# First feed-forward matrix as seven half-size products, its granules alternating in pairs with those of the second matrix

## The chip, the cores and the metric

The kernel runs on one core of one Trainium2 chip. The metric is device time in microseconds (us) of one execution: 1838.39 us as the median of three runs (1836.11 to 1846.52). All durations below come from one profiled execution, which took 1839.03 us in all and whose instructions span 1837.2 us. The engines are TensorE (PE; its weight loads stand apart as PEld), VectorE (DVE), ScalarE (ACT), GpSimd (POOL) and SyncE (SP, which here only issues DMAs).

## The reference, cut to what matters

One step of a decoder trunk runs on 256 prompt rows and 32 sample rows, so 288 columns in all (`N`), with a model width of 2048. After three recurrent branches and their merge, the last part is a feed-forward layer, and almost half of the kernel's time goes there:

```python
xn = rmsnorm(x, P['g_norm2']) * (1.0 + sc2) + sh2
x = x + gt2 * (jnp.square(jax.nn.relu(xn @ P['w_ff1'])) @ P['w_ff2'])
y = rmsnorm(x, g_final)
```

`w_ff1` is 2048 by 8192, `w_ff2` is 8192 by 2048, both float32. `gt2` is one of six vectors that the conditioning product `silu(c) @ w_ada + b_ada` yields.

## The kernel before

**Precision.** Every float32 matrix and every activation is split into two float16 parts, hi and lo, and a product is made of three float16 products: hi·hi, hi·lo and lo·hi. A weight's hi is written by ACT (a scaled copy), its lo by DVE (`rest`, L134: a scalar_tensor_tensor that reads the raw float32 and the hi, both in SBUF). `rest` also leaves a mark (a sum over its outputs) from which `certificates` later tell whether the fast program is accurate enough; the second copy of the program, behind `tc.If`, is not run.

**Granules.** Weights come in granules of 128 x 1024 float32 (512 KB, one DMA on SP's queue). A granule of the first matrix is 4 row tiles by 256 output columns, one of the second is 2 row tiles by 512. Four granules make a `Block`; each granule is 24 matmuls of 128 x 128 weights against 288 columns (8 tile products times 3). Each matrix has 32 blocks, so there are 256 granules and 6144 matmuls, all at L301.

**Order.** The hidden layer is cut into eight parts (`hb`) of 1024 features. The blocks run ff1(0), ff1(1), ff2(0), ff1(2), ff2(1) and so on: ff1 has four blocks a part, ff2 four more that add into `facc` (`a`, tiles s6 and s7). `feed_forward` goes through the granules ("visits"; the first eight in pairs). At each visit it emits the conversion (hi, lo) of the granule `depth` = 5 further on, then the 24 matmuls of this one, then, where a block ends, its evacuation: for ff1 relu, square and split (L1916 to L1918 and L134), for ff2 the addition to `facc` on DVE (L1940). Inside `in_order` the queues of PE, ACT and DVE keep exactly the order of the code. `convert` also issues the DMA for the granule that takes over the raw buffer it has just read (nine buffers). SP's queue is in program order. POOL is placed by the scheduler.

**Beside it.** The 16 remaining units of the GT2 conditioning product (`gt0`, `gt1`) are worked off during the stage by `every`: "L" loads 1 MB, "C" splits half of it on ACT and DVE (L449, L134), "v" multiplies it on PE (L466). When ff2(6) ends, POOL scales `facc` by gt2 and adds it to x (`half_resid`, L1924 to L1927), so that the last block only adds its own share. Check sums (`certify`) run on DVE and PE at several points.

## Time and profile before

| what | us |
|---|---|
| median of three runs | 1838.39 |
| the profiled execution, in all | 1839.03 |
| its span, first to last instruction | 1837.2 |
| feed-forward, first to last matmul of L301 | 768.0 (1052.7 to 1820.7) |
| PE busy in the span | 1770.3 (96%) |
| DVE busy in the span | 1204.6 |
| ACT busy in the span | 914.6 |
| POOL busy in the span | 216.5 |

A row of a group reads: line, engine, operation, output<-inputs, shape, count, then busy time in us and the mean of one in ns, then the engine's idle time just ahead of them and what ended it. The busy time of a PE group counts overlap once; the mean of one matmul (286 ns) holds its passage through the array, so the distance between two starts is read from a timeline row.

### The profile page before, as it was taken

Reading aid. Unit: us, or ns where it says so; the run is one execution under the profiler, and the core shown is the slowest. Engines: PE = TensorE matmul, PEld = TensorE weight load, DVE = VectorE, ACT = ScalarE, POOL = GpSimd, SP = SyncE. Lnnn points to the kernel's source line nnn. Section 1 sums busy time; section 2 is a strip of 40 time slices with the busy share of each in tenths; the row PEclk is TensorE's granted clock in tenths of the full one; section 3 lists DMA queues with packets and bytes.
Section 4 is the critical chain, followed back from the end, with each engine's and each line's share of the span. In section 5 each row is a group of like instructions: output and inputs, shape, how many; then the busy total and the mean of one; then the engine's idle time right before and its main releaser. Section 6 shows DMA issues by size and latency. Waiting matters only on the chain.

```text
span 1837.2 us, 38589 instructions
## 1 busy us (share of the span) xinstructions
PE 1770.3 (96%) x15792; PEld 1376.8 (75%) x15792; DVE 1204.6 (66%) x2603; ACT 914.6 (50%) x1268; POOL 216.5 (12%) x281
## 2 busy tenths in 40 slices
PE   7999989998898999999999899999999999999996
PEld 5787667786677877677777677777777777777785
DVE  4777855646787467777767776556665666555565
ACT  5334374555455455465556555554444444343443
POOL 0002201110125010001113510000000000000171
PEclk9999999999999999999999999999999999999998
DMA  9999766647755459977778546566656655555541
GB/s 393 414 409 335 260 227 247 216 157 247 237 194 187 163 196 297 323 259 252 254 271 316 221 165 204 201 200 220 203 197 206 216 198 197 179 177 181 180 154 54
DMA packets 113291, 422.97 MB, mean 230 GB/s; under 512 B 11649, under 2 KB 11937, under 8 KB 109905
## 3 DMA queue, kind: packets, MB, share of 16 engines
q1 hardware_dynamic: 97744, 364.18, 56.7%
q0 software_dynamic: 10608, 39.64, 6.3%
q10 hardware_dynamic: 4752, 16.60, 2.4%
q8 instruction: 125, 2.05, 0.4%
q14 instruction: 62, 0.50, 0.1%
HBM read 403.56 MB, written 16.81 MB: 229 GB/s over the span
## 4 chain that ended last, share of the span: by engine, by line
PE 63%; DVE 2%; DMA 2%; issue 1%; ACT 1%; POOL 0%; DVEq 0%; POOLq 0%; ACTq 0%
PE mm L301 32%; PE mm L237 19%; PE pi L301 8%; PE pa L466 1%; DMA st<-mC 1%; DMA o_C_s<-st 1%; DVE pair L134 0%; PE px L1629 0%; PE px L1639 0%; PE px L1715 0%; DVE st L1718 0%; PE pi L1698 0%; DMA xl<-wf 0%; DVE s L2051 0%; PE px L1570 0%
## 5 line engine op out<-in xcount | busy, mean ns | idle before, releaser
L237 PEld LDWEIGHTS <-pair 128*128 128x128 f16 x6528 | 633.1, 98 | 218.3 <-issue 36.1
L301 PEld LDWEIGHTS <-pair 128*128 128x128 f16 x6144 | 600.8, 98 | 160.2 <-issue 8.3
L237 PE MATMUL mm<-x,pair 128*128 128x288 f16 x4320 | 563.7, 287 | 14.1 <-ACT s L714 6.1
L134 DVE SCALAR_TENSOR_TENSOR pair<-raw,pair 128x1024 f16<-128x1024 f32 x250 | 308.3, 1235 | 213.7 <-ACT pair L224 119.5
L301 PE MATMUL mm<-hx,pair 128*128 128x288 f16 x2472 | 321.0, 286 | 0.0
L301 PE MATMUL mm<-z,pair 128*128 128x288 f16 x2448 | 312.7, 287 | 4.4 <-ACT z L1899 3.7
L134 DVE SCALAR_TENSOR_TENSOR pair<-xl,pair 128x1024 f16<-128x1024 f32 x165 | 202.7, 1229 | 132.6 <-ACT pair L224 73.3
L224 ACT ACTIVATE pair<-raw 128x1024 f16<-128x1024 f32 x163 | 171.5, 1054 | 202.3 <-PE mm L237 118.9
L134 DVE SCALAR_TENSOR_TENSOR pair<-s,pair 128x1024 f16<-128x1024 f32 x113 | 140.1, 1241 | 122.6 <-ACT pair L210 122.3
L224 ACT ACTIVATE pair<-xl 128x1024 f16<-128x1024 f32 x109 | 114.9, 1054 | 157.3 <-PE mm L237 89.4
L210 ACT ACTIVATE pair<-s 128x1024 f16<-128x1024 f32 x113 | 119.0, 1054 | 142.4 <-PE mm L301 105.5
L210 ACT ACTIVATE pair<-raw 128x1024 f16<-128x1024 f32 x87 | 91.5, 1054 | 124.0 <-PE mm L301 84.3
L237 PE MATMUL mm<-y,pair 128*128 128x288 f16 x768 | 99.8, 290 | 6.0 <-ACT ag L1361 6.0
L210 ACT ACTIVATE pair<-xl 128x1024 f16<-128x1024 f32 x56 | 58.8, 1054 | 80.0 <-PE mm L301 68.4
L237 PE MATMUL mm<-mrg,pair 128*128 128x288 f16 x768 | 95.3, 286 | 0.0
L1924 POOL TENSOR_SCALAR s<-s,mod 128x256 f32<-128x256 f32 x16 | 14.8, 927 | 665.7 <-DVE s L1940 665.7
L301 PE MATMUL pi<-hx,pair 128*128 128x288 f16 x600 | 89.8, 286 | 0.0
L301 PE MATMUL pi<-z,pair 128*128 128x288 f16 x624 | 85.0, 286 | 0.0
L134 DVE SCALAR_TENSOR_TENSOR ag<-ag,uh 128x1024 f16<-128x1024 f32 x34 | 45.8, 1360 | 19.3 <-ACT uh L449 19.3
L237 PE MATMUL mm<-s,pair 128*128 128x288 f16 x384 | 51.9, 294 | 5.3 <-ACT s L1361 5.3
L237 PE MATMUL px<-x,pair 128*128 128x288 f16 x288 | 42.1, 287 | 4.0 <-DVE pair L134 3.3
L449 ACT ACTIVATE uh<-ag 128x1024 f16<-128x1024 f32 x34 | 34.9, 1043 | 21.8 <-DMA ag<-wada 21.8
(476 smaller groups left out, 1610.0 us busy)
## 6 DMA issues: line engine op xcount, KB each, us to landing
raw<-win SPq DMA_DIRECT2D x115, 512.0 KB, 4.8
s<-wf SPq DMA_DIRECT2D x113, 512.0 KB, 3.5
raw<-wf SPq DMA_DIRECT2D x87, 512.0 KB, 3.4
xl<-win SPq DMA_DIRECT2D x77, 512.0 KB, 5.0
xl<-wf SPq DMA_DIRECT2D x56, 512.0 KB, 3.4
s<-wq SPq DMA_DIRECT2D x20, 1024.0 KB, 12.9
xl<-wada SPq DMA_DIRECT2D x16, 1024.0 KB, 6.2
s<-wada SPq DMA_DIRECT2D x13, 1024.0 KB, 6.5
```

What stands on the lines that cost most here:

```text
L134: return V.scalar_tensor_tensor(dst, src, scale, hi if fast else hi.bitcast(F32), op, ALU.subtract, accum_out=mark(w))
L210: pace["hi"] = S.activation(hi, raw, AF.Copy, scale=WS)
L224: pace["hi"] = S.activation(hi, raw, AF.Copy, scale=WS)
L237: pace["last"] = T.matmul(ps, w[:, kk, ms], x, start=k == k0 and i == 0, stop=k == kt - 1 and i == 2)
L301: pace["last"] = T.matmul(self.ps[m][:, :N], a[:, kk, m * P:(m + 1) * P], x, start=k == 0 and i == 0, stop=k == 4 * self.kg - 1 and i == 2)
L449: S.activation(h, w, AF.Copy, scale=AS)
L466: pace["prod"] = T.matmul(ps[32 * j:32 * j + 32, a:a + 256], silp[:, 32 * k:32 * k + 32], v[:, j], start=q == i == n == 0, stop=q == KT // ...
L1924: G.tensor_scalar(a[:, 0:NP], a[:, 0:NP], mod[:, GT2, k, 0:1], None, ALU.mult)
```

## The change

**Seven products.** For 27 of the 32 blocks of the first matrix (all but hb 0 and the first of hb 1) a granule's four row tiles by two column tiles are taken as two 2 x 2 grids of 128 x 128 tiles, and the 288 columns as two halves of 144 (`H`). Instead of the eight products of a grid's four weight tiles with the two column halves, seven are made, from sums of weight tiles and sums of activation tiles (Strassen's scheme in Winograd's form). A granule `Seven` has 7 x 2 x 3 = 42 matmuls of 144 columns for 24 of 288. The weights are repacked on the host (`quadrants`), so that a granule's raw tile holds the four quadrants side by side.

**Sums.** Per granule POOL makes four sums of 128 x 256 in the raw tile (in `fetch`), which grows from 1024 to 1792 columns; ACT and DVE then split all 1792. The sums of the activations are made once (`differences`, on POOL, DVE and ACT, into the tile `xl`). The seven products land in two px banks and the pi bank; `seven`'s evacuation puts four sums together on DVE, then ACT makes relu and two squares over 576 columns and DVE splits 576.

**Order and buffers.** The 27 blocks alternate with the blocks of ff2: two granules of the one, two of the other. Granules with sums have three raw tiles (s2, s3, s8), the others the three `raw` buffers. The parts go round ten tiles (two for a granule with sums, one for another), `depth` is 6, and evacuations are emitted one visit later, behind that visit's conversion.

**Smaller edits.** GT2's product goes from float16 parts back to float32 on PE (no split on ACT and DVE), a unit every 14 visits. `half_resid` is called per block in the last 20 visits. All check sums are made in the last 15 visits.

The diff, cut to its core:

```diff
     def certificates():
-        yield from certify(0, mixed[0], 8.0)
-        yield from certify(704, mixed[1], 2.0 ** -3)
...
+        upto = list(marks)
+        yield from certify(704, upto[1], 2.0 ** -3)
+        yield from certify(0, upto[0], 8.0)
...
+    H = N // 2
+    S3, A11, A12, A22, S1, S2, S4 = range(0, 1792, 256)
+    class Seven:
...
+        def multiply(self, g, hi, lo):
+            if self.ps is None:
+                self.ps = misc(), misc(), longp()
+            for a, b, i in ((A11, 0, 0), (S2, 0, 2), (A12, 0, 1), (S3, 1, 1), (S1, 1, 0), (A22, 2, 1), (S4, 2, 0)):
+                p = self.ps[b][:, H * i:H * i + H]
+                for j in range(2):
+                    xh, xl = self.forms(a, 2 * g + j)
+                    c = a + P * j
+                    for n, (w, x) in enumerate(((hi, xh), (hi, xl), (lo, xh))):
+                        pace["last"] = T.matmul(p, w[:, c:c + P], x, start=g == j == n == 0 and a in (A11, S3, A22),
...
-        if fast:
+        if fast and kind != GT2:
             return cond_parts(name, load, 2, lambda _, pv: ada_finish(kind)(h, pv))
...
+    def differences(k, E):
+        z = sp.tile([P, 1028], F32, tag="st", name=nm("st"), bufs=2)
+        e = [z[:, H * i:H * i + H] for i in range(5)]
+        E.tensor_tensor(out=z[:, 0:2 * N].rearrange("p (a n) -> p a n", a=2), in0=zh[:, 2 * k:2 * k + 2, :], in1=zl[:, 2 * k:2 * k + 2, :], op=ALU.add)
+        for o, a, b in ((4, 3, 1), (1, 1, 0), (3, 3, 1), (2, 2, 3)):
+            G.tensor_tensor(out=e[o], in0=e[a], in1=e[b], op=ALU.subtract)
+        h, l = (zt[0][:, i, k, :] for i in range(2))
+        S.activation(h, z[:, H:5 * H], AF.Copy)
+        rest(l, z[:, H:5 * H], 1.0, h)
...
+    def seven(hb, b):
+        def ev(pa_, pb, pc):
...
+            S.activation(o, pa_[:, 0:H], AF.Copy)
+            V.tensor_tensor(out=q[:, 0:5:4], in0=o.unsqueeze(1).to_broadcast([P, 2, H]), in1=two(pa_, 1), op=ALU.add)
+            V.tensor_tensor(out=q[:, 1:4:2], in0=q[:, 4:5].to_broadcast([P, 2, H]), in1=two(pb, 0), op=ALU.add)
+            V.tensor_tensor(out=q[:, 1:3], in0=q[:, 1:4:2], in1=two(pc, 0), op=ALU.add)
+            V.tensor_tensor(out=q[:, 3], in0=q[:, 3], in1=pb[:, 0:H], op=ALU.add)
+            hi, lo = (flat(t[:, 2 * b:2 * b + 2, :]) for t in hx[hb % 2])
+            S.activation(c, c, AF.Relu, scale=1.0 / (WS * ZS))
+            S.activation(hi, c, AF.Square)
+            S.activation(c, c, AF.Square)
+            rest(lo, c, 1.0, hi)
...
+        for hb in range(1, 8):
+            second = list(ff2(hb - 1))
+            for b in range(int(hb == 1), 4):
+                w = seven(hb, b)
+                for g in (0, 2):
+                    order += [(w, g), (w, g + 1), (second[b], g), (second[b], g + 1)]
+        order += [(b, g) for b in ff2(7) for g in range(4)]
...
+        Q.dma_start(t[:, 0:1024], b.w[b.blk, b.g0 + g])
         raws[i] = t
+        if isinstance(b, Seven):
+            q = lambda c: t[:, c:c + 256]
+            for o, x, op, y in ((S1, S3, ALU.add, A22), (S3, A11, ALU.subtract, S3), (S2, S1, ALU.subtract, A11), (S4, A12, ALU.subtract, S2)):
+                G.tensor_tensor(out=q(o), in0=q(x), in1=q(y), op=op)
...
+            if isinstance(order[i][0], Seven):
+                pairs[i] = [next_parts()[:, 0:1792] for _ in range(2)]
+                to_parts(raws.pop(i)[:, 0:1792], *pairs[i])
...
+            for j in then_.get(i, ()):
+                fetch(j)
...
-    depth = 5 if fast else 3
+    depth = 6 if fast else 3
...
+                finish_later()
                 multiply(ss)
...
+            if fast and s >= total - 20 and s % 4 == (total - 20) % 4 and s < total - 4:
+                b = (s - total + 20) // 4
+                for k in range(4 * b, 4 * b + 4):
+                    half_resid(x2[k // 8][:, k % 8, :], facc[k // 8][:, k % 8, :], k)
...
-        slots.update(ids=("x", None), n=0)
-        every("L . . . . . C . C . . v", skip=8)
+        slots.update(ids=(None,), n=0)
+        every("L . v" + 11 * " .", skip=8)
```

What stands on DVE before, in the middle of the feed-forward stage (L134 is a split, L1918 and the split into hx are an ff1 block's evacuation, the L134 on ag belongs to GT2):

```order
L134 SCALAR_TENSOR_TENSOR ag_14825,gd<-ag_14825,uh_15005 128x1024
L134 SCALAR_TENSOR_TENSOR pair_15073,gd<-s_1284_12240,pair_15073 128x1024
L134 SCALAR_TENSOR_TENSOR pair_15101,gd<-xl_111,pair_15101 128x1024
L134 SCALAR_TENSOR_TENSOR pair_15129,gd<-xl_111,pair_15129 128x1024
L1918 TENSOR_TENSOR t_1549_15146<-t_1548_15145 128x288
L134 SCALAR_TENSOR_TENSOR hx_12238,gd<-t_1549_15146,hx_12238 128x288
L1918 TENSOR_TENSOR t_1551_15164<-t_1550_15163 128x288
L134 SCALAR_TENSOR_TENSOR hx_12238,gd<-t_1551_15164,hx_12238 128x288
```

What stands on DVE in the changed kernel, in the middle of the alternating stretch (L1966 to L1969 are the four sums of a seven-product block, the split into hx its end, L1995 an addition to `facc`; sources s are raw tiles with sums, sources raw those of the second matrix):

```order
L134 SCALAR_TENSOR_TENSOR pair_12208,gd<-raw_13805,pair_12208 128x1024
L134 SCALAR_TENSOR_TENSOR s_1289_12209,gd<-raw_13932,s_1289_12209 128x1024
L1966 TENSOR_TENSOR st_14146<-st_14146,px_13883 128x2x144
L1967 TENSOR_TENSOR st_14146<-st_14146,px_13884 128x2x144
L1968 TENSOR_TENSOR st_14146<-st_14146,pi_13885 128x288
L1969 TENSOR_TENSOR st_14146<-st_14146,px_13884 128x144
L134 SCALAR_TENSOR_TENSOR hx_12199,gd<-st_14146,hx_12199 128x576
L134 SCALAR_TENSOR_TENSOR uh_12210,gd<-s_1282_12202,s_1289_12209 128x1792
L134 SCALAR_TENSOR_TENSOR uh_12212,gd<-s_1280_12200,uh_12211 128x1792
```

Two splits of 1792 columns and two of 1024 now follow each other, a block's split of 576 stands ahead of the two long ones, and every two granules an evacuation stands in the row.

What stands on POOL in the changed kernel at that place, where there was nothing before (with the engines that each row waits for; a wait for DVE is for the raw tile to be read, one for Pool for the sum before):

```order
L2059 TENSOR_TENSOR s_1280_12200<-s_1280_12200 128x256 [waits DMAHW6_49,DVE_49]
L2059 TENSOR_TENSOR s_1280_12200<-s_1280_12200 128x256 [waits Pool_49]
L2059 TENSOR_TENSOR s_1280_12200<-s_1280_12200 128x256
L2059 TENSOR_TENSOR s_1281_12201<-s_1281_12201 128x256 [waits DMAHW7_49,DVE_49]
L2059 TENSOR_TENSOR s_1280_12200<-s_1280_12200 128x256 [waits Pool_49]
```

The sums of the next tile are mixed with the last one of the tile before.

More of the change, by code (lines that the diff above doesn't have):

```diff
@@ L1908, in trunk, with ff1 @@
     tail = {}
-    def ff1(hb):
-        for b in range(4):
+    def ff1(hb, bs=range(4), banks=bank):
+        for b in bs:
             def ev(m, p, b=b):
@@ L1940, in ev @@
                     V.tensor_tensor(out=a, in0=a, in1=p, op=ALU.add)
-                    if hb == 6:
+                    if hb == 6 and not fast:
                         half_resid(x, a, k)
@@ L1947, in ev @@
                     S.activation(x, x, AF.Copy, scale=Pm("gf")[:, k:k + 1])
[L1948 to L1956 removed]
+            yield Block(io["wf2"], b, 4 * hb, 512, lambda k: (x[0][:, k, :], x[1][:, k, :]), ev, *((lambda: pm.tile([P, 512], F32, tag="mm", name=nm("mm")),) if fast else ()))
@@ new lines, in trunk @@
+    if fast:
+        own = lambda: pm.tile([P, 512], F32, tag="mm", name=nm("mm"))
+        blocks = [next(ff1(0, (b,), misc if b == 2 else own)) for b in range(4)] + list(ff1(1, (0,), misc)) + [next(ff2(0))]
+    else:
+        blocks = []
+        for hb in range(9):
+            if hb < 8:
+                blocks.extend(ff1(hb))
+            if hb:
+                blocks.extend(ff2(hb - 1))
+    order = [(b, g) for g in range(4) for b in blocks[0:2]] + [(b, g) for b in blocks[2:] for g in range(4)]
@@ L1957, in trunk @@
+    plain = len(order)
+    if fast:
+        for hb in range(1, 8):
[5 more added lines that the diff above has]
+        order += [(b, g) for b in ff2(7) for g in range(4)]
     visits = [(2 * i, 2 * i + 1) for i in range(4)] + [(i,) for i in range(8, len(order))]
     total = len(order)
+    raws, pairs, later = {}, {}, []
@@ L1960, in trunk @@
+    wide = [flat(slot(i)) for i in (2, 3, 8)] if fast else []
     homes = [flat(slot(3))[:, 0:2048]]
     if fast:
-        homes = [flat(slot(8))[:, 0:2048], extra["xl"][:, 0:2048]] + homes
+        homes = [wide[i][:, 0:2048] for i in (2, 0, 1)]
     homes = [t[:, a:a + 1024] for t in homes for a in range(0, t.shape[1], 1024)] + [None] * 3
-    raws, pairs, places = {}, {}, []
+    home, before, after, n = [], {}, {}, [0, 0]
+    for i in range(total):
+        if isinstance(order[i][0], Seven):
+            h = n[0] % 3
+            n[0] += 1
+        elif not fast:
+            h = 3 + (i - 3) % len(homes) if i > 2 else None
+        else:
+            h = 3 + (i - 3) % len(homes) if 2 < i < 12 else None
+        home.append(h)
@@ new lines, in trunk, with next_parts @@
+    started, then_ = places()
+    if fast:
+        ring_ = [wp.tile([P, 2048], F16, tag="pair", name=nm("pair"), bufs=5) for _ in range(5)]
+        ring_ += [t.bitcast(F16) for t in (flat(slot(9))[:, 0:1024], flat(slot(9))[:, 1024:2048])] if False else []
+        nine = flat(slot(9))
+        ring_ += [nine[:, 1024 * i:1024 * i + 1024].bitcast(F16) for i in range(2)]
+        ring_ += [sp.tile([P, 2048], F16, tag="uh", name=nm("uh"), bufs=3) for _ in range(3)]
+        turn_ = [0]
+    def next_parts():
+        turn_[0] += 1
+        return ring_[(turn_[0] - 1) % len(ring_)]
@@ L1994, in multiply @@
                     b.multiply(g, *t, (m,), range(b.kg))
-                b.evac(m, b.ps[m][:, :N])
-    depth = 5 if fast else 3
+                if plain <= ss[0] < total - 16 and fast:
+                    later.append(lambda b=b, m=m: b.evac(m, b.ps[m][:, :N]))
+                else:
+                    b.evac(m, b.ps[m][:, :N])
+    depth = 6 if fast else 3
     okc = sc([P, 16], "oks", 1)
-    now = [0]
     def feed_forward():
@@ L2019, in feed_forward @@
                     made += 1
+                finish_later()
                 multiply(ss)
-                now[0] = s
-                if fast and v >= 12:
-                    next(proof, None)
+                if fast and 4 <= v < 20 and v % 2 == 0:
+                    if not zt:
+                        zt.append(extra["xl"].bitcast(F16).rearrange("p (i k c) -> p i k c", i=2, k=8))
+                    differences(v // 2 - 2, V if v % 4 else G)
+                if fast and s >= total - 15:
+                    next(proof, None)
+                    if s % 2:
+                        next(proof, None)
+            if fast and s >= total - 20 and s % 4 == (total - 20) % 4 and s < total - 4:
+                b = (s - total + 20) // 4
+                for k in range(4 * b, 4 * b + 4):
+                    half_resid(x2[k // 8][:, k % 8, :], facc[k // 8][:, k % 8, :], k)
             yield
-    result, mixed, proof = [], list(marks), certificates()
+    result, proof = [], certificates()
     with in_order():
-        for i in range(len(homes)):
+        for i in started:
             fetch(i)
```

124 lines of the change are left out of this document (92 added, 32 removed).

## The prediction

> **What bounds the kernel now.** The page comes first: its span, the engines' totals and the costliest groups.
>
> ```profile
> span 1837.2 us, 38589 instructions
> PE 1770.3 (96%) x15792; PEld 1376.8 (75%) x15792; DVE 1204.6 (66%) x2603; ACT 914.6 (50%) x1268; POOL 216.5 (12%) x281
> L301 PEld LDWEIGHTS <-pair 128*128 128x128 f16 x6144 | 600.8, 98 | 160.2 <-issue 8.3
> raw<-wf SPq DMA_DIRECT2D x87, 512.0 KB, 3.4
> s<-wf SPq DMA_DIRECT2D x113, 512.0 KB, 3.5
> ```
>
> PE is busy 96% of the span and DVE two thirds. These are averages, so the second view is the busy time inside the feed-forward stage, the third the waits in its middle, the fourth the chain that ends last.
>
> ```profile
> 1052.70:1820.70 768.00, 765.88 (x6369) 606.82 (x6369) 470.08 (x1009) 366.07 (x477) 53.62 (x76) 1.00 0.56 185
> DVE pair L134 <- ACT pair L210: 245.0, 202, 2.4
> ACT pair L210 <- PE mm L301: 230.5, 139, 2.5
> by line: PE mm L301 69.8%; PE pi L301 18.1%; DVE s L2051 2.8%; PE pa L660 1.8%; DVE s L2055 0.7%; issue 0.6%; DVE t L666 0.4%; DVE row L670 0.4%; PE px L146 0.4%; ACT rsc L668 0.2%; DVE rsc L669 0.2%; DVEq L2058 0.1%; DVEq L666 0.0%
> ```
>
> Of 768.0 us PE is busy for 765.9, DVE for 470 (61%), ACT for 366, POOL for 54, at full clock (1.00). DVE waits for ACT's hi, and ACT waits for matmuls, that is for a part tile to be read. So the chain runs in a ring that PE closes, and from 1700 us to the end 88% of it is L301. PE bounds this stage alone; DVE has 298 us to spare. The change takes from PE and gives to DVE and POOL.
>
> **PE's term.** Two rows of PE's timeline give the distance of two matmuls.
>
> ```profile
> 1091.42 14.86 PE L301 MATMUL mm<-z,pair 128*128 128x288 f16 x120
> 1106.12 1.63 PE L301 MATMUL pi<-z,pair 128*128 128x288 f16 x12
> 571.64 1.88 PEld L1534 LDWEIGHTS px<-s,s 128*128 128x128 f32 x16
> 571.76 1.95 PE L1534 MATMUL px<-s,s 128*128 128x128 f32 x16
> 573.54 0.65 PE L237 MATMUL mm<-y,pair 128*128 128x288 f16 x4
> ```
>
> 120 matmuls of 288 columns start within 14.70 us: 122.5 ns each, 2.94 us for a granule's 24. A matmul of 144 columns isn't in the trace. From below it is half, 61.3 ns. The nearest row is the float32 one: 16 matmuls of 128 columns from 571.76 to 573.54 are 111 ns each. Read as two passes over 128 columns these are 55.6 each, and a line through (128, 55.6) and (288, 122.5) gives 62.3 at 144; I take 62.5. The end from above is the weight load: a group's mean is 98 ns, and if loads did not overlap, that would be the distance. The same float32 rows speak against it: 16 loads there start 111 ns apart, under matmuls that keep that pace.
>
> A block of the alternating stretch (four granules of each kind) now costs 8 x 2.94 = 23.52 us of PE. Afterwards it costs 4 x 42 x 62.5 ns + 4 x 2.94 = 10.50 + 11.76 = 22.26. The saving is 1.26 a block, 34 us over 27. That is all there is to gain; a seventh of half the work goes, and shorter matmuls give a little back.
>
> The Trainium skill ("TensorE: Matmul & The Clock Gate", section "Back-to-back issue gap") has a rule against this change: a sustained stream of load and matmul keeps about 81 ns at 128 columns and 131 at 512. By an estimate on the line between these, 144 columns take 83 ns and a block 4 x 42 x 83 ns + 11.76 = 25.7 us. On the same line 288 columns would take 102 ns; the trace's 122.5 differs, so I give the rule little.
>
> **DVE's term.** Durations come from two splits that follow each other, and from the stage's groups.
>
> ```profile
> 1790.22 1.23 DVE L134 SCALAR_TENSOR_TENSOR pair<-xl,pair 128x1024 f16<-128x1024 f32 x1 [2.43 <-ACT pair L210]
> 1791.37 1.22 DVE L134 SCALAR_TENSOR_TENSOR pair<-xl,pair 128x1024 f16<-128x1024 f32 x1
> L134 DVE SCALAR_TENSOR_TENSOR pair<-raw,pair 128x1024 f16<-128x1024 f32 x84 | 103.5, 1235 | 91.6 <-ACT pair L210 91.6
> L134 DVE SCALAR_TENSOR_TENSOR hx<-t,hx 128x288 f16<-128x288 f32 x64 | 29.3, 458 | 7.4 <-DVE t L1918 0.9
> L1940 DVE TENSOR_TENSOR s<-s,mm 128x288 f32<-128x288 f32 x77 | 30.9, 447 | 0.0
> 1392.45 1.18 DVE L1940 TENSOR_TENSOR s<-s,mm 128x288 f32<-128x288 f32 x3
> L210 ACT ACTIVATE pair<-raw 128x1024 f16<-128x1024 f32 x84 | 88.3, 1054 | 117.5 <-PE mm L301 84.3 <-PE pi L301 29.4 <-DMA s<-wf 3.8
> L1917 ACT ACTIVATE hx<-t 128x288 f16<-128x288 f32 x64 | 28.3, 443 | 2.0
> ```
>
> Split to split is 1.15 us at 1024 columns. The means at 1024 and 288 (1235, 458) give 1.056 ns a column, so 1792 take 1.15 + 0.81 = 1.96, and 576 take 0.458 + 0.304 = 0.76, less the 0.08 of overlap, 0.68. In the same way ACT's slope is 0.83 ns a column: a hi of 1792 takes 1.69, a pass over 576 0.68, and 0.71 with the hand-over. An addition to `facc` takes (1.18 - 0.45) / 2 = 0.37 in a row.
>
> A block then has on DVE, in the order shown above:
> - four splits of 1792 and four of 1024: 7.84 + 4.60 = 12.44;
> - four additions to `facc` in a row: 1.46;
> - the four sums of the seven-product evacuation, each on the one before: 3 x 0.48 + 0.33 = 1.77;
> - the split into hx behind ACT's three passes. What is queued behind it on DVE waits with it, the next two long splits and through them PE: 3 x 0.71 = 2.13, then 0.68;
> - the next hi, which ACT makes only behind those passes: 1.69, of which 0.68 lies under that split: 1.0.
>
> The sum is 12.44 + 1.46 + 1.77 + 2.13 + 0.68 + 1.0 = 19.5 us, below PE's 22.26. If that were all, the change would win.
>
> **The port.** A stretch of an earlier stage shows POOL's additions beside DVE, with DVE's operation alone behind it; the last stage shows a split under an addition of 288 columns.
>
> ```profile
> 539.41 4.72 DVE L842 SCALAR_TENSOR_TENSOR s<-s,par,s 128x253 f32<-128x253 f32 x5
> 540.59 0.74 POOL L862 TENSOR_TENSOR s<-s,par 128x256 f32<-128x256 f32 x1
> 541.41 0.78 POOL L863 TENSOR_TENSOR s<-s 128x256 f32<-128x256 f32 x1
> 542.27 0.72 POOL L862 TENSOR_TENSOR s<-s,par 128x256 f32<-128x256 f32 x1
> 543.07 0.79 POOL L863 TENSOR_TENSOR s<-s 128x256 f32<-128x256 f32 x1
> 545.20 1.26 DVE L842 SCALAR_TENSOR_TENSOR s<-s,par,s 128x255 f32<-128x255 f32 x3
> 546.39 1.21 DVE L134 SCALAR_TENSOR_TENSOR pair<-raw,pair 128x1024 f16<-128x1024 f32 x1
> 1743.28 4.04 POOL L1927 TENSOR_TENSOR s<-s,s 128x288 f32<-128x288 f32 x4
> 1744.93 1.73 DVE L134 SCALAR_TENSOR_TENSOR pair<-raw,pair 128x1024 f16<-128x1024 f32 x1 [1.71 <-ACT pair L210]
> ```
>
> Alone, three DVE operations with two SBUF inputs take 1.19 us, 0.40 each; beside POOL five take 4.72, 0.94 each, and additions start 0.83 apart. The two take turns: one addition costs a waiting DVE operation 0.83 - 0.40 = 0.43. The split beside L1927 is 1.73 long for 1.23, so it lost 0.50 to an addition of 288 columns. A split of 1.96 that is under way holds POOL back in turn. A block has nine such DVE operations (eight splits and the one into hx), so the port costs between 0 and 9 x 0.45 = 4.05 us; additions come in spells of four, so I take five of nine, **2.1**.
>
> The Trainium skill ("SBUF — State Buffer", section "Who interferes with whom") calls the port pair of DVE and GpSimd an exclusive lock. Here an addition of 0.72 to 0.79 us cost DVE only 0.43, which bears out the turns but not a hold over its whole length.
>
> **The late tile.** A granule with sums now goes: DMA 3.5 us (the page's row), four additions 4 x 0.7 = 2.8 without waits, about 3.3 in which three splits hold them up (two of 1.15, one of 1.96, the longest partly past), then hi 1.69. That is 11.3 us from the split that frees a raw tile to the split that needs its next content. With three raw tiles, that split stands half a block further down in DVE's row. The half without the seven-product evacuation holds 2 x 1.96 + 2 x 1.15 + 1.46 = 7.7 of work, 8.6 with its share of the port: 2.7 too little, and with a landing later than the median **2.9**. The other half holds about 13 and hides it. Behind that late split stand the `facc` additions, which free the four banks of the second matrix, so PE waits at the start of a new ff2 block. The bounds are 0 (POOL far ahead) and 3.
>
> A block so takes 19.5 + 2.1 + 2.9 = **24.5 us** on DVE, against 22.26 on PE and 23.52 now.
>
> **Smaller terms.** GT2's product, `half_resid` and the opening:
>
> ```profile
> 1052.70:1820.70 768.00, 8.11 (x208) 4.29 (x208) 1.00 0.56 185
> L466 PE MATMUL pa<-uh,silp 128*32 128x256 f16 x104 | 6.7, 276 | 0.0
> L418 PE MATMUL pa<-s,mod 128*32 128x256 f32 x32 | 1.9, 382 | 0.0
> L1924 POOL TENSOR_SCALAR s<-s,mod 128x256 f32<-128x256 f32 x16 | 14.8, 927 | 665.7 <-DVE s L1940 665.7
> L1927 POOL TENSOR_TENSOR s<-s,s 128x288 f32<-128x288 f32 x16 | 16.1, 1038 | 0.0
> ```
>
> The first row is that window for L466 alone: 208 matmuls, at 6.7 / 104 = 64 ns some 13.4 us. The float32 form stands in the trace at 1.9 / 32 = 59 ns, so this edit costs **0** (-4 to +4); DVE and ACT lose 26 halves of a split, which were beside PE. `half_resid` puts some 31 us (these two rows) on POOL, part of it now among the last additions: **+2** (0 to 8). `differences` puts eight POOL chains beside the opening's `xn` work: **+2** (0 to 6). The check sums only move, 0.
>
> **The sum.** 27 x 24.5 = 661.5, the 40 plain granules 117.6, and 3 for GT2 where PE isn't what is waited for: 782.1 for 768.0, +14; with +2 and +2, +18 on the profiled execution's 1839.03, which lies 0.6 above the median. **1857 us.**
>
> **Rivals.**
> 1. *The additions hide and PE stays the bound.* DVE's 61% and POOL's 7% of the stage speak for it; what is queued behind the hx split and behind a late tile speaks against. It decides once DVE's block is under 22.26 + 0.5 for GT2: 27 x 22.26 = 601, + 117.6 + 15 for GT2 + 2 = 736 for 768, so 1807; with a few waits left, 22.9 to 23.2 a block, 1814 to 1822. Chance 0.31, faster.
> 2. *The forecast*, a block of 24.0 to 25.2: 1843 to 1877. Chance 0.39.
> 3. *Smaller waits* (port 1.5, late tile 2.3): a block of 23.3 is 629 + 117.6 + 3 + 4 = 754, so 1825; up to 23.9, 1841. Chance 0.18, of it 0.05 faster.
> 4. *The port is held for the whole addition* (0.7 for 0.43, five times 1.35 a block), and with POOL in turn behind it the late tile comes 0.7 later: 26.5 a block, 1911. The split that lost 0.50 beside an addition of 1.0 speaks against. Chance 0.09, slower. It is what the page on SBUF in the Trainium skill would lead to.
> 5. *Weight loads don't hide under 144 columns*: at 98 ns a block is 4 x 42 x 98 ns + 11.76 = 28.2 on PE, 1957. It decides from 70 ns on, where a block's 23.5 equals today's. The float32 loads 111 ns apart speak against. Chance 0.03, slower. By the figure of the Trainium skill's section on the back-to-back gap, 25.7 a block, an estimate would be 1901.
>
> **How the numbers follow.** A measurement of this kernel tells about 0.5% from no change (three runs lay between 1836.11 and 1846.52), so 1830 to 1848 counts as the same. Of the forecast's 0.39, 0.07 lie there and 0.32 above; with rivals 4 and 5 slower has 0.44. The same has 0.07 and rival 3's 0.13, 0.20. Faster has 0.31 and 0.05, 0.36. The range of 1812 to 1892 leaves out the best of rival 1 and most of 4 and 5; the forecast's own is 1843 to 1877.
>
> **What would show it.** In the profile after, the start-to-start distance of the 144-column matmuls (62.5 ns), the distance between the same places of two blocks (24.5 us), splits of 1792 with a mean well over 2.04 us while the additions run and at 2.04 where none does, and waits of PE at the third granule of a group of eight, where the `facc` banks come free. If PE never waits in the alternating stretch, or if waits go to DMA instead of POOL, the prediction is wrong.

## The result, and the profile after

The changed kernel takes 1924.24 us (median of four runs, 1920.84 to 1928.98) against 1839.61 before: ratio 1.0457, 95% interval 1.0419 to 1.0495. It is slower by 85 us. 1857 was predicted, with a range up to 1892. Of the kernels below, two had one execution each in a slow state at a lower clock (2251.42 us at 0.751 and 2023.45 us at 0.847), and their times are medians of the other three.

The page of the changed kernel, its busy time over the feed-forward stage (first to last of its matmuls) and over the alternating stretch (columns: length, then busy time of PE, PEld, DVE, ACT and POOL, PE's clock, DMA share, GB/s), and PE's waits in the middle of that stretch:

```profile
span 1922.0 us, 42910 instructions
PE 1772.7 (92%) x17728; PEld 1423.8 (74%) x17728; DVE 1325.9 (69%) x2537; ACT 955.4 (50%) x1244; POOL 687.6 (36%) x749
1051.40:1905.00 853.60, 767.64 (x8305) 654.14 (x8305) 597.42 (x953) 411.68 (x458) 533.08 (x544) 0.96 0.53 167
1140.10:1847.40 707.30, 633.25 (x7275) 551.47 (x7273) 497.74 (x695) 341.09 (x337) 470.93 (x459) 0.96 0.56 178
PE pa L434 <- DMA ag<-wada: 27.7, 11, 4.0
PE mm L296 <- DVE s L1995: 14.1, 9, 2.8
```

The stage grew from 768.0 to 853.6 us; all of the loss lies in it. From the first to the last matmul of 144 columns it is 707.3 us, and with the end of the last ff2 block the 27 blocks take 715.6, so 26.5 each, where PE's own work is 22.26. No engine is busy all the time: PE 90%, DVE 70%, POOL 67%. So something is in a ring with waits. PE's timeline shows that the matmuls themselves are as fast as predicted:

```profile
1629.23 6.04 PE L296 MATMUL mm<-hx,pair 128*128 128x288 f16 x48
1635.11 0.54 PE L317 MATMUL px<-z,pair 128*128 128x144 f16 x6
1635.49 0.54 PE L317 MATMUL px<-xl,pair 128*128 128x144 f16 x6
1635.86 0.54 PE L317 MATMUL px<-z,pair 128*128 128x144 f16 x6
```

Twelve matmuls of 144 columns start within 0.75 us (1635.11 to 1635.86): 62.5 ns each, weight loads hidden. The 34 us are really saved on PE. Read alone, the waits above accuse the load of the GT2 units (`ag`), and the chain agrees: between 1200 and 1780 us it gives that load 12.3% and the sums on POOL 6.5%.

```profile
by line: PE mm L296 25.5%; PE px L317 16.8%; DMA ag<-wada 12.3%; issue 10.5%; POOL s L2059 6.5%; PE pi L317 5.9%; DMA s<-wf 4.5%; ACT pair L202 3.5%; DVE pair L134 3.1%; PE pa L434 2.4%; DVE uh L134 2.0%; ACT uh L202 1.4%; DVE s L134 1.0%; 
```

The first experiments test that reading against the prediction's.

### The profile page after: what moved, and what is told of

Read it like the earlier page. It is cut to its first block, busy times and chain, and to the rows that moved or that the text cites. A ratio compares the mean times of both kernels' runs of the same rounds, so it can differ in the third digit from the quotient of the medians.

```text
span 1922.0 us, 42910 instructions
## 1 busy us (share of the span) xinstructions
PE 1772.7 (92%) x17728; PEld 1423.8 (74%) x17728; DVE 1325.9 (69%) x2537; ACT 955.4 (50%) x1244; POOL 687.6 (36%) x749
## 4 chain that ended last, share of the span: by engine, by line
PE 40%; DMA 8%; DVE 7%; issue 6%; POOL 5%; ACT 4%; DVEq 0%; SPq 0%; ACTq 0%; POOLq 0%
PE mm L229 20%; PE mm L296 10%; PE px L317 5%; DMA ag<-wada 4%; POOL s L2059 4%; DMA s<-wf 2%; DVE pair L134 2%; PE pi L317 2%; ACT pair L202 2%; DMA st<-mC 1%; DVE uh L134 1%; POOL st L1946 1%; DVE s L134 1%; PE pa L434 1%; ACT uh L202 1%
## 5 line engine op out<-in xcount | busy, mean ns | idle before, releaser
L229 PEld LDWEIGHTS <-pair 128*128 128x128 f16 x6528 | 632.4, 98 | 211.3 <-issue 31.5
L2059 POOL TENSOR_TENSOR s<-s 128x256 f32<-128x256 f32 x432 | 448.6, 1058 | 225.5 <-DMA s<-wf 183.6
L134 DVE SCALAR_TENSOR_TENSOR pair<-raw,pair 128x1024 f16<-128x1024 f32 x237 | 305.9, 1300 | 133.7 <-ACT pair L216 122.3
L296 PEld LDWEIGHTS <-pair 128*128 128x128 f16 x1824 | 179.7, 99 | 71.4 <-issue 25.3
L296 PE MATMUL mm<-hx,pair 128*128 128x288 f16 x1584 | 203.3, 288 | 15.4 <-DVE s L1995 14.1
L134 DVE SCALAR_TENSOR_TENSOR pair<-xl,pair 128x1024 f16<-128x1024 f32 x109 | 134.5, 1234 | 74.0 <-ACT pair L216 73.2
L317 PEld LDWEIGHTS <-pair 128*128 128x128 f16 x2422 | 167.2, 99 | 11.2 <-issue 9.6
L202 ACT ACTIVATE pair<-s 128x1792 f16<-128x1792 f32 (+1 forms) x67 | 110.8, 1669 | 104.7 <-POOL s L2059 64.0
L296 PEld LDWEIGHTS <-uh 128*128 128x128 f16 x1056 | 104.8, 100 | 43.5 <-issue 15.8
L296 PE MATMUL mm<-hx,uh 128*128 128x288 f16 x912 | 118.6, 290 | 13.9 <-ACT s L1991 7.6
L134 DVE SCALAR_TENSOR_TENSOR pair<-s,pair 128x1792 f16<-128x1792 f32 (+1 forms) x45 | 97.3, 2169 | 46.7 <-ACT pair L202 46.7
L317 PE MATMUL px<-xl,pair 128*128 128x144 f16 x1038 | 94.5, 229 | 0.0
L317 PEld LDWEIGHTS <-uh 128*128 128x128 f16 x1190 | 88.6, 100 | 2.6 <-issue 1.6
L317 PEld LDWEIGHTS <-s 128*128 128x128 f16 x924 | 83.0, 101 | 8.6 <-issue 8.0
L296 PEld LDWEIGHTS <-s 128*128 128x128 f16 x672 | 67.2, 101 | 27.0 <-issue 8.8
```

The costliest lines, as they stand in the source:

```text
L134: return V.scalar_tensor_tensor(dst, src, scale, hi if fast else hi.bitcast(F32), op, ALU.subtract, accum_out=mark(w))
L202: pace["hi"] = S.activation(hi, raw, AF.Copy, scale=WS)
L229: pace["last"] = T.matmul(ps, w[:, kk, ms], x, start=k == k0 and i == 0, stop=k == kt - 1 and i == 2)
L296: pace["last"] = T.matmul(self.ps[m][:, :N], a[:, c:c + P], x, start=k == 0 and i == 0, stop=k == 4 * self.kg - 1 and i == 2)
L317: pace["last"] = T.matmul(p, w[:, c:c + P], x, start=g == j == n == 0 and a in (A11, S3, A22), stop=g == 3 and j == 1 and n == 2, skip_gro ...
L2059: G.tensor_tensor(out=q(o), in0=q(x), in1=q(y), op=op)
```

## The experiments

Each kernel ran beside the kernel before on the same chip; times are medians, and ratios are to the kernel before. That one took 1838.07 to 1840.40 us in the several rounds, so 2 us between kernels of different rounds say nothing.

**Which wait counts.** Four kernels: the GT2 load earlier; `half_resid` held behind the last sum; both; the earlier load with the sums left out.

```diff
-        every("L . v" + 11 * " .", skip=8)
+        every("L . . . . . v" + 7 * " .", skip=8)
```

> The changed kernel with one edit: a GT2 unit's load is issued six visits ahead of its product instead of two (the pattern of 14 visits stays). Theory A (PE waits for a load issued too late): in the changed kernel's trace the 13 units put 49.1 us between the matmuls around them, 12.4 of it the products themselves (208 x 59 ns), and the matmuls behind each wait run at a lower clock for some 8 us in all; without the wait 37 to 45 us go, 1879 to 1887 us, and no wait of PE for the load is left. Rival B (DVE and POOL bound the alternating blocks, as the prediction has it): PE's time at the loads lets them catch up, so the waits for the facc banks take its place, and less than 15 us go: above 1909.

Measured: 1922.78 us, ratio 1.0443 (1.0426 to 1.0461): 1.5 us less than the changed kernel. Theory A is refuted, and rival B holds. The load's waits are gone, and PE waits for the `facc` banks instead:

```profile
PE mm L296 <- DVE s L1995: 36.6, 18, 3.8
PE mm L296 <- ACT s L1991: 1.6, 2, 1.3
```

14.1 us of that wait became 36.6 (both 1200 to 1740 us). The GT2 wait was no cost of its own: while PE stood at it, the slower ring caught up.

```diff
-                G.tensor_tensor(out=q(o), in0=q(x), in1=q(y), op=op)
+                pace["add"] = G.tensor_tensor(out=q(o), in0=q(x), in1=q(y), op=op)
...
+                with tc.issue_after(pace["add"].ins):
+                    for k in range(4 * b, 4 * b + 4):
+                        half_resid(x2[k // 8][:, k % 8, :], facc[k // 8][:, k % 8, :], k)
```

> The changed kernel with one edit: half_resid's rows on POOL are held behind the last sum of weight quadrants (no other order changes). Theory A (half_resid's rows stand among the last sums, wait there for DVE's last additions to facc, and the sums behind them come late): the two waits of 7.1 us near 1793 and 1827 and what follows them go, some 20 to 23 us, 1901 to 1904. Rival (half_resid is then late itself, and the last blocks wait for it): no gain or a loss, 1915 to 1935.

> Both edits, the earlier GT2 load and half_resid behind the last sum. Theory A: they add up, 57 to 68 us less than the changed kernel, 1856 to 1867. If the blocks are bound by DVE and POOL (rival B), less than 40 go, above 1884.

Measured: 1913.30 alone (1.0397, 1.0369 to 1.0426), 1909.01 with the earlier load (1.0376, 1.0344 to 1.0408). `half_resid` among the last sums costs 11 to 14 us, about half of the 20 to 23 that the waits there suggested, and the two edits don't add up to theory A's 57 to 68: rival B holds again. The two waits at L1966 (first row, earlier load alone, 1780 to 1860 us) go, and the wait for the banks stays (second and third row, without and with the edit):

```profile
PE px L317 <- DVE st L1966: 10.6, 2, 5.3
PE mm L296 <- DVE s L1995: 6.8, 3, 2.5
...
PE mm L296 <- DVE s L1995: 7.1, 3, 3.3
```

```diff
-                G.tensor_tensor(out=q(o), in0=q(x), in1=q(y), op=op)
+                pass
```

> The earlier GT2 load, and the four sums per granule on POOL left out (their columns hold what the tile held before; splits and products run as they are). What is left of the waits for the facc banks (22 us in the changed kernel's trace between 1200 and 1780), the wait near 1153 and those near the end should go, because all hang on a tile with sums that comes late: some 40 to 55 us less than the kernel with the earlier load alone, 1830 to 1845, blocks of 22.3 us and PE without a wait in the alternating stretch. If the prediction's two terms for the port and the late tile (5 us a block) stand once the GT2 waits are gone, the difference is over 80 us. If DVE's own work bounds the blocks, less than 15 us go.

Measured: 1826.59 us (0.9926, 0.9906 to 0.9946), 96 us less than with the sums: more than the 40 to 55 expected from the waits alone, over 80 as the prediction's two terms have it. (The kernel leaves the sums out, so it doesn't compute the layer; the next one doesn't either.) PE waits 0.6 us for the banks between 1200 and 1740. DVE's own work, 448 of 618.9 us, doesn't bind; the sums on POOL do, and the next question is how.

**Port or late tile.** The sums run, load the port, and write to spare columns, so that no split waits for them.

```diff
-                G.tensor_tensor(out=q(o), in0=q(x), in1=q(y), op=op)
+                G.tensor_tensor(out=q(1792), in0=q(x), in1=q(y), op=op)
```

> The earlier GT2 load, and POOL's four sums per granule run as before but write to spare columns of the same tile, so that no split waits for them; the columns of the sums hold what the tile held before, so the products are made of other weights. The port is loaded as before, the late tile is gone. Theory L (the late tile is the larger part): DVE's steady block of 25.65 us loses the 3.75 us of waiting and PE bounds at 22.3 to 23.3: 1835 to 1865, within 30 us above the kernel without sums (1827). Rival P (the port itself costs the time: splits of 2.2 to 2.5 us for 2.03): above 1885.

Measured: 1860.63 us (1.0118, 1.0093 to 1.0143). So 62 of the 96 us are the wait for the sums, the late tile, at the end with what `half_resid` adds to it; 34 are the rest, the port and POOL's own rows in the opening and at the end. Counted by matmuls in the traces, the 22 blocks in the middle (the third to the 24th) take 561.0 us with the sums, 514.6 with the sums beside and 501.9 without. The groups of a sum on POOL and of one of the long splits (1200 to 1740 us; first with the earlier load alone, then with the sums beside, then without sums) show that the port can't be the larger part:

```profile
L2059 POOL TENSOR_TENSOR s<-s 128x256 f32<-128x256 f32 x340 | 366.1, 1097 | 171.4 <-DMA s<-wf 154.3 <-DVE pair L134 7.8
L134 DVE SCALAR_TENSOR_TENSOR pair<-s,pair 128x1792 f16<-128x1792 f32 x34 | 75.9, 2240 | 37.9 <-ACT pair L202 37.9
...
L2059 POOL TENSOR_TENSOR s<-s 128x256 f32<-128x256 f32 x362 | 507.3, 1417 | 21.1 <-DMA s<-wf 4.6
L134 DVE SCALAR_TENSOR_TENSOR pair<-s,pair 128x1792 f16<-128x1792 f32 x38 | 92.3, 2446 | 4.9 <-ACT pair L202 4.9
...
L134 DVE SCALAR_TENSOR_TENSOR pair<-s,pair 128x1792 f16<-128x1792 f32 x37 | 74.5, 2023 | 22.2 <-issue 10.6 <-ACT pair L202 10.0 <-PE mm L296 1.5
```

With the sums beside, a sum takes 1.42 us and a split 2.45, both longer than in the slower kernel, since they meet more often. Yet the time is 62 us less, and since the port is loaded more here, the 34 us are rather too much for it than too little. What went is DVE's idle time before the long splits (37.9 to 4.9 us in this group).

**The steady block.** Behind the earlier load the blocks repeat almost exactly: from one set of `facc` additions to the next most take 25.65 us, as most do in the changed kernel too. DVE's timeline of one, then ACT, POOL and SP around its wait (POOL's row of eight sums, and the third of them alone):

```profile
1612.07 2.02 DVE L134 SCALAR_TENSOR_TENSOR uh<-s,uh 128x1792 f16<-128x1792 f32 x1
1614.02 1.54 DVE L1995 TENSOR_TENSOR s<-s,mm 128x288 f32<-128x288 f32 x4
1615.47 1.22 DVE L134 SCALAR_TENSOR_TENSOR pair<-raw,pair 128x1024 f16<-128x1024 f32 x1
1616.62 1.74 DVE L134 SCALAR_TENSOR_TENSOR pair<-raw,pair 128x1024 f16<-128x1024 f32 x1
1618.29 2.53 DVE L134 SCALAR_TENSOR_TENSOR pair<-s,pair 128x1792 f16<-128x1792 f32 x1
1624.54 2.30 DVE L134 SCALAR_TENSOR_TENSOR s<-s,pair 128x1792 f16<-128x1792 f32 x1 [3.71 <-ACT pair L202]
1626.77 1.74 DVE L134 SCALAR_TENSOR_TENSOR s<-raw,s 128x1024 f16<-128x1024 f32 x1
1628.44 1.73 DVE L134 SCALAR_TENSOR_TENSOR uh<-raw,uh 128x1024 f16<-128x1024 f32 x1
1630.11 0.44 DVE L1966 TENSOR_TENSOR st<-st,px 128x288 f32<-128x288 f32 x1
1634.19 0.97 DVE L134 SCALAR_TENSOR_TENSOR hx<-st,hx 128x576 f16<-128x576 f32 x1 [2.18 <-ACT st L1973]
1635.77 2.03 DVE L134 SCALAR_TENSOR_TENSOR uh<-s,uh 128x1792 f16<-128x1792 f32 x1 [0.61 <-ACT uh L202]
1639.67 0.45 DVE L1995 TENSOR_TENSOR s<-s,mm 128x288 f32<-128x288 f32 x1
...
1622.81 1.70 ACT L202 ACTIVATE pair<-s 128x1792 f16<-128x1792 f32 x1 [7.65 <-POOL s L2059]
...
1615.99 8.96 POOL L2059 TENSOR_TENSOR s<-s 128x256 f32<-128x256 f32 x8 [7.10 <-DMA s<-wf]
1618.90 2.50 POOL L2059 TENSOR_TENSOR s<-s 128x256 f32<-128x256 f32 x1
...
1612.18 2.27 SPq L2054 DMA_DIRECT2D s<-wf  x2
```

A block is 1639.67 - 1614.02 = 25.65 us. The raw tile is free at 1612.07; its next load is issued at 1612.18 and its sums start at 1615.99; three of them stand beside three splits (1.22, 1.74 and 2.53); ACT's hi starts at 1622.81 and DVE's split at 1624.54, 12.5 us after the tile was free. DVE came to that place after 8.7 us and idled 3.7.

**The order on POOL.** In the changed kernel a granule's fourth sum stands behind the next granule's first. In this run POOL keeps the order of the code (the earlier load too).

```diff
-            if i.engine in (mybir.EngineType.PE, mybir.EngineType.Activation, mybir.EngineType.DVE):
+            if i.engine in (mybir.EngineType.PE, mybir.EngineType.Activation, mybir.EngineType.DVE, mybir.EngineType.Pool):
```

> The earlier GT2 load, and POOL in the order of the code through the whole stage (the four sums of a granule behind each other, not the next granule's first ahead of the last one's fourth; the opening's second_norm rows and half_resid where the code has them). Theory L (in a steady block of 25.65 us DVE idles 3.75 us for the second long split of a pair, because its tile comes late over POOL): one sum of 0.72 less on that path, 27 x 0.7 = 19 us, and 14 us at the end as half_resid alone gave, some 5 in the opening: 1877 to 1893. Rival D (DVE's own work with the port bounds the block, and the idle time only moves): no more than the 14 to 19 of end and opening, 1903 to 1909.

Measured: 1903.06 us (1.0360, 1.0333 to 1.0388), at the edge of rival D's range. But the steady block is shorter by 0.58 us, most of what one sum takes (0.72), as theory L says: 1582.37 - 1557.30 = 25.07 us, and DVE's wait is 3.14 for 3.71. Less than expected came from the whole: in the opening PE's wait for L1991 grew from 10.5 to 14.3 us and the one for L1915 from 7.5 to 10.3, which takes 6.6 us back.

```profile
1557.30 1.54 DVE L1995 TENSOR_TENSOR s<-s,mm 128x288 f32<-128x288 f32 x4
...
1567.26 2.30 DVE L134 SCALAR_TENSOR_TENSOR pair<-s,pair 128x1792 f16<-128x1792 f32 x1 [3.14 <-ACT pair L202]
...
1582.37 1.18 DVE L1995 TENSOR_TENSOR s<-s,mm 128x288 f32<-128x288 f32 x3
```

**One by one.** Three kernels that should have given each tile more time by alternating single granules:

```diff
-                for g in (0, 2):
-                    order += [(w, g), (w, g + 1), (second[b], g), (second[b], g + 1)]
+                for g in range(4):
+                    order += [(w, g), (second[b], g)]
```

> The earlier GT2 load, and the two kinds of granule alternate one by one instead of two by two; nothing is removed. A raw tile with sums is then needed again after three quarters of a block (14 us of DVE's work) instead of half a block (8.6) and a whole one in turn. Theory L: the late tile's 3.75 us a block go, DVE's block is 21.9 and PE bounds at 22.3 to 23.3 us: 63 to 90 us less than the kernel with the earlier load alone, 1833 to 1860. Rival D: the port and POOL's time stay, a block of 24.9 or more, above 1900.

> One by one, the earlier GT2 load and POOL in the order of the code. Theory L: as the kernel that alternates one by one, and 14 us less at the end, 5 to 10 in the opening: 1815 to 1840. Rival D: above 1885.

> One by one, with the GT2 load two visits ahead as in the changed kernel. If theory L holds, the blocks are bound by PE, nothing is left to take the waits for the load over, and the 13 units cost what the trace of the changed kernel shows at them: 30 to 45 us more than one by one with the earlier load. If the blocks are still bound by DVE and POOL, under 8 us.

Measured: 1968.01, 1969.93 and 1963.63 us (ratios 1.0699, 1.0727 and 1.0693, each within 0.004). These are 41 to 47 us slower than two by two with the earlier load, and no theory had it. In the trace of the first, theory L's own wait is gone: between 1200 and 1740 us ACT's hi waits 7.8 us for POOL's sums, where it was 102.1 (64.3 + 22.5 + 15.3). PE meets another wait instead, the one for the `facc` banks (first row, the same window, 36.6 us two by two; then DVE in one block):

```profile
PE mm L296 <- DVE s L1995: 60.0, 18, 3.8
...
1563.42 1.25 DVE L134 SCALAR_TENSOR_TENSOR hx<-st,hx 128x576 f16<-128x576 f32 x1 [2.18 <-ACT st L1973]
...
1566.27 1.54 DVE L1995 TENSOR_TENSOR s<-s,mm 128x288 f32<-128x288 f32 x4
```

The edit changed a second thing. Two by two, two granules with sums (5.3 us of PE) lie between the end of an ff2 block and the next one, which needs its banks; one by one it is a single one (2.6 us), and the additions that free the banks stand close behind the seven-product evacuation with its wait for ACT. This is read from the order of the code and the rows; no run tests it alone. So these runs show that the late tile can be hidden, but not what that is worth. As a side result, the late GT2 load again cost nothing where another wait binds.

**The opening.** With POOL in the code's order and the earlier load, the first granules' sums were put behind `second_norm`, and the copy and split of each difference one visit later; then the differences were also moved to visits 4 to 11, ahead of all sums.

```diff
+            if i in first3:
+                held_sums.append(sums)
...
-                if fast and 4 <= v < 20 and v % 2 == 0:
+                if fast and 4 <= v < 12:
```

> The earlier GT2 load, POOL in the order of the code, and two edits of the opening: the sums of the first three granules follow second_norm instead of standing among its rows, and the copy and split that end each difference of activations are issued one visit later, so that ACT's row doesn't wait for POOL's chain of four. If the opening's 25 us beyond before (between the first matmul and some 1200 us) come from these two waits, 12 to 22 us less than the kernel with POOL in the order of the code (1903): 1881 to 1891. If they come from the long splits themselves, under 5.

> As the run with the edits of the opening, but the eight differences of activations are made in visits 4 to 11, one in each, before any sum of weight quadrants is on POOL (the first three granules' sums follow in visit 11), instead of visits 4 to 18 among them. If the opening's loss beyond before (some 20 us between the first matmul and 1210 us) comes from differences and sums waiting for each other on POOL, with ACT's and DVE's rows behind them, 8 to 16 us less than that run (1899): 1883 to 1891. If it is the late tile itself, which the first blocks meet as the later ones do, under 4: above 1895.

Measured: 1898.98 (1.0319, 1.0294 to 1.0345) and 1895.27 us (1.0311, 1.0292 to 1.0330): 4 and 8 us less than with POOL's order alone. The gains of 12 to 22 and then 8 to 16 more didn't come, and both times fall on the other branch (under 5; above 1895): the late tile is met in the opening too. PE's waits there (1040 to 1200 us; before, changed kernel, the second of these) show that one wait gave way to another. The last row is the one in ACT's row that stands ahead of the 7.6 us in the changed kernel.

```profile
PE mm L301 <- ACT z L1899: 3.7, 2, 2.3
...
PE mm L296 <- ACT s L1991: 7.6, 1, 7.6
PE mm L296 <- ACT z L1915: 7.1, 3, 3.2
...
PE mm L296 <- ACT pair L202: 4.6, 2, 4.2
PE mm L296 <- DVE pair L134: 4.3, 3, 3.2
PE mm L296 <- ACT z L1915: 3.9, 3, 1.8
...
1150.53 0.68 ACT L1948 ACTIVATE xl<-st 128x576 f16<-128x576 f32 x1 [10.98 <-POOL st L1946]
```

**Fewer blocks with sums.** If a block with sums is late by 2.8 us and a plain one has time over, six visits of lead should carry it. Every other block of the 27 was made plain (13 with sums), with the opening's first edits; the same with the late GT2 load; then with the differences in visits 4 to 11; then 17 with sums, two of three in a row.

```diff
-                w = seven(hb, b)
+                w = seven(hb, b) if (4 * hb + b) % 2 == 0 else next(ff1(hb, (b,), misc))
```

> As the run with the edits of the opening, but every other block of the 27 is made in plain form (13 with seven products, the first and the last of the 27 plain). A block with sums needs 25.1 us of DVE and POOL for 22.26 of PE, a plain one some 14 of DVE for 23.52 of PE; six visits of lead carry the 2.8 us over. Then PE bounds nearly all of it: 13 x 1.26 = 16 us less than before, some 5 to 10 of the opening left: 1826 to 1838. If the waits stay in the blocks with sums (2.8 us x 13 = 36), 1855 to 1870.

> As the run before it, but the GT2 load two visits ahead as in the changed kernel. Where PE bounds, nothing takes the wait for the load over: 30 to 45 us more than the run before it. If the wait is hidden again, under 8 us.

> Every other block with seven products (13 of 27), as before, with the differences in visits 4 to 11. In the run without that, 11 us of waits beyond before were left in the opening and none behind it. If they go, 5 to 10 us less than it: 1830 to 1835, 0.2 to 0.5% faster than the kernel before; GT2's float32 products still cost 6 us more than before. If not, 1838 to 1842.

> 17 of the 27 blocks with seven products, two of three in a row, with the differences in visits 4 to 11. Two such blocks run 2 x 2.8 us late; six visits of lead (some 16 us) carry that, and a plain block has 9 us of DVE's time over to recover. Then PE still bounds: 4 x 1.26 = 5 us less than the run with every other block, 1825 to 1830. If the waits come back in the second of two such blocks, 8 x 2.8 = 22 us more than it: 1852 to 1857.

Measured: 1840.37 (1.0001, 0.9985 to 1.0017), 1848.58 (1.0052, 1.0037 to 1.0068), 1844.69 (1.0039, 1.0026 to 1.0053) and 1837.68 us (0.9996, 0.9986 to 1.0007). The window from 1200 to 1780 us of the first has PE busy throughout:

```profile
1200.00:1780.00 580.00, 580.00 (x5801) 482.79 (x5799) 401.33 (x652) 279.98 (x301) 208.51 (x204) 1.00 0.61 196
```

The same holds for two blocks in a row. So the lead carries the late tile. The first, third and fourth are slower than hoped all the same (1826 to 1838, 1830 to 1835 and 1825 to 1830). Two other things kept them from gaining. In the first, PE saves 13 x 1.26 = 16 us, but the stage up to the second alternating block takes 135.0 us for 124.6 before, and GT2's float32 products cost PE more than the float16 ones did. A GT2 unit stands between the two rows of each pair, the matmuls ahead of it and those behind it (first the kernel before, with 6 matmuls of 122.5 ns ahead, then this one, with 24):

```profile
1164.15 0.90 PE L301 MATMUL pi<-hx,pair 128*128 128x288 f16 x6
1165.54 1.64 PE L301 MATMUL mm<-hx,pair 128*128 128x288 f16 x12
...
1284.18 3.10 PE L296 MATMUL mm<-hx,s 128*128 128x288 f16 x24
1288.22 3.11 PE L296 MATMUL mm<-hx,uh 128*128 128x288 f16 x24
```

From start to start, less the matmuls ahead, a unit takes 1.39 - 0.74 = 0.65 us before and 4.04 - 2.94 = 1.10 here, so 6 us more for 13 units. The late GT2 load cost 8 us, not 30 to 45; 7 of them lie up to the second alternating block (142.1 us for 135.0), and in the middle only 1.5 us of waits for it are left. A reason may be SP's queue, in which a load stands behind fetches that wait for DVE's splits: once DVE is no longer the last, the queue runs ahead. No run tests that. With every other block, crowding the differences into eight visits was worse than the even spread.

Last, the differences in every third visit from 4 to 25, the first sums in visit 19, and `second_norm` as the scheduler placed it; with 17 blocks, and with 19, three of four in a row.

```diff
-                if fast and 4 <= v < 20 and v % 2 == 0:
+                if fast and 4 <= v < 28 and v % 3 == 1:
```

> 17 of 27 blocks with seven products as in the run before, but the differences are spread (one in every third visit from 4 to 25), the first granules' sums follow in visit 19, and second_norm's rows on POOL stand where the scheduler put them in the kernel before. The run before had no wait behind 1200 us and 20 us of waits and slow matmuls in the opening, against 5 in the kernel before. If those come from the differences crowding POOL and DVE, 10 to 15 us go: 1823 to 1830, 0.5 to 0.8% faster than the kernel before. If the opening needs them whatever their place, 1835 to 1840.

> As the run before it with 19 of 27 blocks, three of four in a row. Three such blocks run 3 x 2.8 = 8.4 us late, within the lead of six visits (16 us): another 2 x 1.26 = 2.5 us less, 1821 to 1828. If the lead is used up in the third block, 6 x 2.8 = 17 us more than the run before it.

Measured: 1832.86 (0.9971, 0.9957 to 0.9986) and 1843.05 us (1.0016, 1.0004 to 1.0027). The first is the only kernel with all its sums in place that beats both others, by 0.3%, less than expected. PE saves 17 x 1.26 = 21 us; the stage up to the second alternating block keeps 10 of it (134.4 us for 124.6), GT2's products 6, the last 16 granules 2 (49.1 for 47.1). One wait of 6.9 us stands out in the opening: ACT copies the first ff2 bank only behind two long his and the copy of a difference, for which it waits 10.2 us on POOL.

```profile
PE mm L296 <- ACT s L1993: 6.9, 1, 6.9
PE mm L296 <- ACT z L1915: 3.2, 2, 1.8
```

In the second, waits for the banks come back behind 1200 us (10.0 us in eight places). With 10 us more than the kernel ahead it lies between its two branches, nearer to the one with 17: three in a row are more than the lead carries.

## Why the prediction was wrong

The mechanism of the blocks was right, but three terms of the sum were too small: the block, the opening and the end. Counted by matmuls, the stage divides as follows (in us; the forecast is made of 24 and 16 granules at 2.94, blocks at 24.5 and its 2 + 2):

| part of the stage | before | forecast | changed | earlier load | sums beside | sums left out |
|---|---|---|---|---|---|---|
| 24 plain granules, blocks 1 and 2 | 124.6 | 121.6 | 145.0 | 144.7 | 144.3 | 133.1 |
| blocks 3 to 24 | 525.2 | 539.0 | 565.1 | 561.0 | 514.6 | 501.9 |
| blocks 25 to 27, 16 plain granules | 118.0 | 122.5 | 143.2 | 147.5 | 126.4 | 121.4 |

With 3 for GT2 the forecast is 786 us; the changed kernel took 853. Of what it lacked, 23 us lie in the first part, 26 in the second and 21 in the third.

- **PE's term** held to the digit: 62.5 ns, 22.26 us a block. Rival 5 and the page's rule on load and matmul streams in the Trainium skill ("TensorE: Matmul & The Clock Gate", section "Back-to-back issue gap"; 83 ns by the estimate) are excluded by the rows of 0.54 us. The prediction's "a seventh of half the work" should read an eighth, and by the same additions as its 1957 for rival 5 the 25.7 us a block give 1890, not 1901.
- **The ring of DVE, POOL and SP** bounds the blocks, as forecast (rival 1 fell), and the late tile is the larger part, which the sums beside and the sums left out show. Only the sizes were off. DVE's own terms were 19.5 and are 19.4 in the steady block (1.46 + 4.60 + 7.84 + 1.90 + 2.18 + 0.68 + 0.69). The port was 2.1 and is 2.5 (the splits' rows less 1.15, 1.95 and 0.68 each). The late tile was 2.9 and is 3.75: 12.5 us from free to split for 11.3, of which 0.7 is the next granule's first sum that stands ahead of the fourth (0.58 by the run in the code's order). The order on POOL showed this, and the text ahead of the prediction quoted it; the sum left it out. 25.65 for 24.5 us, and 25.69 on the average of blocks 3 to 24, is 26 us over these 22.
- **The end** was 2 (0 to 8); holding `half_resid` back gave 11 to 14. Its rows on POOL wait for DVE's `facc` additions, and the sums queued behind them wait too: the prediction counted its busy time, not what stood behind its wait. With the ring's excess in the last three blocks the part is 21 us above its forecast.
- **The opening** was 2 (0 to 6), and the part is 23 us above its forecast. Some 12 of the 20 us above the kernel before hang on the sums (144.7 with them, 133.1 without). The changed kernel's trace shows 14.7 us of waits of PE there (two rows above) for 3.7 before, and PE's clock is 0.92 there for 0.99. The longest, 7.6 us, can be followed back: ACT copies the first ff2 bank behind a long hi, this behind the copy of a difference, and for that it stood 11 us for POOL, where the difference came behind sums whose tile POOL had awaited for 8.2 us. The prediction counted the time of the chains on POOL, not the row of ACT that waits for them. The other 8 us stay open; moving the sums and the differences moved the waits more than it removed them. What is shown is that it depends on their place: 1837.68 (0.9996) became 1832.86 (0.9971) by spreading them and leaving `second_norm` where the scheduler has it.
- **GT2** was priced by its products alone, at 0 (-4 to +4). These cost PE 6 us more, as the rows above show: the prediction divided the busy time of a group by its count (64 and 59 ns), but a matmul of the float16 group lasts 276 ns by its row, and in a unit four start every 0.12 us. What counts is the time from neighbour to neighbour. Its load's lead of two visits against a landing of 7.3 us was missed, and the trace then showed 28 us of waits, the wait for a DMA that the prediction had named as a sign of being wrong; yet removing them gave 1.5 us. In the changed kernel the price was right by luck: PE had that time over.
- **Rival 4** (the port held for a whole addition) gave 1911, nearest to the result, and its hold is what the rows show. The sum that starts at 1618.90, beside a split, ends 0.58 us behind it, and a split that starts while a sum runs loses most of what is left of that sum. This agrees with the exclusive lock of the section "Who interferes with whom" of the page "SBUF — State Buffer" in the Trainium skill. The prediction had read turns without a hold from rows of short operations. Rival 4's price was wrong all the same: a split lost 0.5 us to a sum, not 0.7, and the tile came 0.7 later by the order on POOL, not by the port. That its number is nearest is luck: it puts into the blocks (26.5 for 25.65) what came in the opening and at the end. With the sums beside, the port is loaded more and the kernel is 62 us faster.

## What to carry to other kernels

A wait on the engine that is busy most may only be where the slack of a slower ring shows: take it away and see whether another takes its place before counting it. When work moves to an engine that feeds others, follow one buffer from free to free (load, each step on each queue, what stands ahead of it there) and compare that with the other engine's work in between; totals of busy time (here 70% and 67%) don't show it. Follow the waits in an in-order queue as well: what a row costs is also what stands behind it. A ring that is some us too slow can be carried by lead, if blocks that need it alternate with blocks that don't.

## What was not expected of the hardware

A POOL sum and a DVE split exclude each other, and the price is uneven. With the earlier load, between 1200 and 1740 us, 121 sums start while a split is under way, and each ends 0.58 to 0.59 us behind that split, however long it was (2.50 us for 0.72 in the row above): nearly all of its work comes after. The 22 splits of 1024 columns during which a sum only starts take 1.22 us, as alone. Those that start while a sum is running lose what is left of it, less some 0.14 us: 0.52 of 0.65 at 1024 columns, 0.43 of 0.57 at 1792, 0.22 of 0.36 at 576 (medians of 56, 45 and 21). So a split loses at most some 0.5 us to one sum, while a sum loses up to the length of a split. When sums met splits most often, a sum's mean rose to 1.42 us and POOL was busy 507 of 540 us for work that takes 0.72 x 362 = 261 us alone.
